# Attention heads: softmax denominator applied to the mixed values, and the mixing product turned around

## The chip, the cores and the metric

The kernel runs on one core of a Trainium2 chip. The core has five engines with a queue of instructions each: PE (TensorE, the matrix unit), DVE (VectorE), ACT (ScalarE), POOL (GpSimd) and SP (SyncE, which here only starts DMAs). The metric is the device time of one execution in microseconds (us), and less is better.

## What is computed

The reference is a trunk of four layers on 256 tokens of width 2048: an S5 state-space mixer, a squared-ReLU MLP of width 8192, windowed attention with 32 query heads and 4 key/value heads of width 64, and a second MLP. Only the attention's core is touched:

```python
scores = jnp.einsum('bnqhgd,bnkhd->bnhgqk', q, k_win).astype(jnp.float32) * scale
...
sink_b = sink.astype(jnp.float32).reshape(1, 1, N_KV_HEADS, GQA_GROUP, 1, 1)
m = jnp.maximum(jnp.max(scores, axis=-1, keepdims=True), sink_b)
p = jnp.exp(scores - m)
denom = jnp.sum(p, axis=-1, keepdims=True) + jnp.exp(sink_b - m)
probs = (p / denom).astype(h.dtype)
out = jnp.einsum('bnhgqk,bnkhd->bnqhgd', probs, v_win)
return out.reshape(bsz, seq, q_w) @ w_o
```

Each query row of each head has one denominator, the sum of its exponentials with that of the head's sink logit. The weights, divided by it, mix the value vectors `v_win`, and the 32 heads' results, side by side, are multiplied with the output matrix `w_o`. As the denominator is the same for all keys of a row, the division can be made on the weights, before the mixing, or on the mixed vector, after it.

## The kernel before, in words

All large products are made in fp32r in three parts (`mm3`, lines 642 to 648): a high half of the activations with the high half of the weights, the low half with it, and the high half with the low half of the weights. Each is one instruction with 128 stationary columns and 512 moving ones; they are called mains here. Weights are streamed: `wload` (L618 to L629) starts a DMA into one of two raw buffers (L622), ACT rounds a copy (the high half, L627), and DVE or POOL subtracts it (the low half, L628), in blocks of 128x2048 or in two halves of 128x1024.

The attention layer runs from about 1139 to 1372 us. Its main work is the query projection, four groups g of 8 heads with 16 slots each (`mains` in `attn_`), and after them the output projection; a slot is 6 mains. Token tiles tt are two of 128 tokens. The work of a group's heads is cut into stages by `attn_head` and spread over the slots of the following group by the table `HS` (L28): for each tt the slot, counted from the group's start, at which each stage is written down. After that a scheduler (Tile's) sets each engine's order from its model of the times; so a stage can stand some slots away from where the table puts it.

The stages of one group and tile:

- `rot`: squares (ACT L945), their sums (DVE L947, L948), a reciprocal root (L189 to L198, L951), and the rotary embedding, DVE L936 and L937 from the projection's bank and POOL L938.
- `turn`: PE transposes the queries (L969), ACT copies them (L971).
- `scores`: 4 products for half of the heads (L980), and DVE adds the mask and takes the row maximum out of the same bank (L984).
- `soft`: DVE L993 to L996, ACT's exponential of 8 heads with their sums (L999), DVE's denominator and its reciprocal (L1000, L1001), and 8 multiplications of the weights `sm` (128 tokens x 256 keys) by it (L1003).
- `flip`, for a pair of heads: 4 PE transposes of the weights (L1009) and ACT's copy `pT` (L1011), keys on the partitions.
- `mix`, for a pair: 4 products (L1018), stationary the values of 64 columns, moving the 128 tokens of `pT`. The result has the head's 64 channels on partitions, the upper head in partitions 64 to 127. After the fourth pair ACT rounds the bank into `aT` (L1023) and DVE writes the low half (L1024), the form in which the output projection needs it.

The 8 banks of PSUM are taken in turn (`bank`, L181): a product that begins a new bank waits until the last reader of that bank's earlier content is done. An fp32 product and an fp32 transpose show as two records each in the trace, so "x8" in the rows is four of them.

Of the kernel before, what the change touches and what calls it, by code (L numbers as in the profile page):

```python
# [9 lines left out]
F32 = mybir.dt.float32  # L10
# [6 lines left out]
P = 128  # L17
# [7 lines left out]
EPS = 1e-6  # L25
KQ = ((0, 1, 2, 3), (0, 1, 2, 3))
NEG = -1e30
HS = ((0, 5, 6, 7, 12, 13, 14, 15, 16), (1, 9, 10, 11, 19, 20, 21, 22, 23))  # L28


OT = 0.2
# [136 lines left out]
class Kernel:  # L168
# [785 lines left out]
    def attn_head(self, pool, g, banks):  # L954

        nc, v, a, pe = self.nc, self.nc.vector, self.nc.scalar, self.nc.tensor
        kT, vt = self.kT, self.vt

        def stages(tt):
            s = {}  # L960

            def rot():
                s["r"] = self.head_r(pool, banks[tt], 8, tt, 0.125, "r8")
                s["q"] = self.rope(pool, banks[tt], 8, 0, tt)

            def turn():
                bk = self.bank()
                for j in range(4):
                    pe.transpose(bk[:, j * P:(j + 1) * P], s["q"][:, j * P:(j + 1) * P], self.ident)  # L969
                s["qT"] = pool.tile([P, 4, P], F32, name="qT")  # L970
                a.copy(s["qT"].rearrange("p h c -> p (h c)"), bk)  # L971
                s["sm"] = pool.tile([P, 8, L], F32, name="sm")
                s["mx"] = self.small.tile([P, 8], F32, name="mx")

            def scores(hq):
                bks = [self.bank() for _ in range(2)]
                for i in range(2):
                    for j in range(2):
                        c = slice(j * 64, (j + 1) * 64)
                        pe.matmul(bks[j][:, i * L:(i + 1) * L], lhsT=s["qT"][c, 2 * hq + i], rhs=kT[c, g], start=True, stop=True)  # L980
                for i in range(2):
                    for j in range(2):
                        h = 2 * (2 * hq + i) + j
                        v.tensor_tensor_reduce(out=s["sm"][:, h], in0=bks[j][:, i * L:(i + 1) * L], in1=self.bias[:, tt],  # L984
                                               scale=1.0, scalar=-3.0e38, op0=ALU.add, op1=ALU.max, accum_out=s["mx"][:, h:h + 1])

            def soft():
                mx, sm = s["mx"], s["sm"]
                snk = self.sink[:, g * 8:(g + 1) * 8]
                nm = self.small.tile([P, 8], F32, name="nm")  # L990
                es = self.small.tile([P, 8], F32, name="es")
                den = self.small.tile([P, 8], F32, name="den")
                v.tensor_mul(mx, mx, s["r"])  # L993
                v.tensor_max(mx, mx, snk)
                v.tensor_scalar_mul(nm, mx, -1.0)
                v.tensor_add(es, snk, nm)  # L996
                a.activation(es, es, AF.Exp)
                for h in range(8):
                    a.activation(sm[:, h], sm[:, h], AF.Exp, scale=s["r"][:, h:h + 1], bias=nm[:, h:h + 1], accum_out=den[:, h:h + 1])  # L999
                v.tensor_add(den, den, es)  # L1000
                v.reciprocal(den, den)  # L1001
                for h in range(8):
                    v.tensor_scalar_mul(sm[:, h], sm[:, h], den[:, h:h + 1])  # L1003

            def flip(hp):
                bk = self.bank()
                for j in range(2):
                    for kt in range(2):
                        pe.transpose(bk[:, (2 * j + kt) * P:(2 * j + kt + 1) * P], s["sm"][:, 2 * hp + j, kt * P:(kt + 1) * P], self.ident)  # L1009
                pT = s["pT", hp] = pool.tile([P, 2, 2, P], F32, name="pT")  # L1010
                a.copy(pT.rearrange("p a b c -> p (a b c)"), bk)  # L1011

            def mix(hp):
                if hp == 0:
                    s["ob"] = self.bank()
                for j in range(2):
                    for kt in range(2):
                        pe.matmul(s["ob"][j * 64:(j + 1) * 64, hp * P:(hp + 1) * P], lhsT=vt[:, kt, g * 64:(g + 1) * 64],  # L1018
                                  rhs=s["pT", hp][:, j, kt], start=(kt == 0), stop=(kt == 1))
                if hp == 3:  # L1020
                    o = self.aT[:, g * 4:(g + 1) * 4, :, tt * P:(tt + 1) * P]
                    ov = s["ob"].rearrange("p (h c) -> p h c", h=4)
                    a.copy(o[:, :, 0], ov)  # L1023
                    v.tensor_sub(o[:, :, 1], ov, o[:, :, 0].bitcast(F32))  # L1024
            return [rot, turn, lambda: scores(0), lambda: (scores(1), soft()),
                    lambda: (flip(0), flip(1)), lambda: (mix(0), flip(2)), lambda: (mix(1), flip(3)), lambda: mix(2), lambda: mix(3)]
        return stages(0), stages(1)

    def proj(self, x, bk, kts, k0, kn):
# [14 lines left out]
    def attn_(self, pool, fin):  # L1044
# [56 lines left out]
        for i, _ in enumerate(mains()):  # L1101
            if i in (1, 2):
                keys(i - 1)
            for tt in range(2):
                for k, at in enumerate(HS[tt]):
                    g, r = divmod(i - 16 - at, 16)
# [246 lines left out]
```

## Time and profile before

| | |
|---|---|
| median of 3 runs | 2124.61 us (2124.23 to 2127.13) |
| profiled execution, its own time | 2126.57 us |
| its span, first to last instruction | 2124.8 us |
| mean granted clock of PE in it | 0.986 |
| attention layer in the span | about 1139 to 1372 us |

Times in the rows count from the span's start. A PE record's duration includes the pipeline, so successive records overlap; what a matmul costs is the step from its start to the next one's start. The granted clock is a share of the full 2.4 GHz; the only other level is 1.2 GHz, so 0.5 in a row or a mean below 1 says how long the lower level held.

### The profile page before, as it was taken

How to read it: one execution, taken by the hardware profiler on the slowest of the kernel's cores; microseconds unless marked ns; L12 is line 12 of the kernel's file. 1: busy time of each engine (PE TensorE's matmuls, PEld its weight loads, DVE VectorE, ACT ScalarE, POOL GpSimd, SP SyncE). 2: the span in 40 equal slices, each digit the busy share in tenths (PEclk: the TensorE clock that was granted, in tenths of full speed). 3: DMA queues.
4: the chain of work that ended last, by engine and by line, in shares of the span. 5: the costliest groups of instructions: out<-in, count | busy, mean ns of one | idle time of the engine just before them, and what ended most of it. 6: DMA issues, size and time to landing. Idle time of an engine off the chain costs nothing.

```text
span 2124.8 us, 33046 instructions
## 1 busy us (share of the span) xinstructions
PE 2034.0 (96%) x13844; PEld 1706.7 (80%) x13844; DVE 1255.5 (59%) x1820; ACT 996.3 (47%) x1233; POOL 334.5 (16%) x245
## 2 busy tenths in 40 slices
PE   3987999999999999999999889999999999999999
PEld 2876778788888888888888667788888888888887
DVE  6899746755555555444457787565555555444444
ACT  5664564444444444433445555545444444344432
POOL 5995850300000000000003340100000000000000
PEclk9998999999999999999999999999999999999999
DMA  3233446455555555655554333255555555555554
GB/s 110 61 95 104 150 175 222 164 186 190 180 193 182 185 189 200 212 187 195 205 194 147 124 119 120 104 196 206 182 195 189 188 197 182 198 196 198 191 188 156
DMA packets 59685, 364.28 MB, mean 171 GB/s; under 512 B 6816, under 2 KB 9152, under 8 KB 19600
## 3 DMA queue, kind: packets, MB, share of 16 engines
q1 hardware_dynamic: 54144, 342.32, 46.3%
q10 hardware_dynamic: 5184, 19.49, 2.8%
q8 instruction: 108, 1.77, 0.3%
q14 instruction: 41, 0.34, 0.0%
q0 software_dynamic: 208, 0.36, 0.0%
HBM read 360.05 MB, written 2.10 MB: 170 GB/s over the span
## 4 chain that ended last, share of the span: by engine, by line
PE 73%; DVE 4%; ACT 2%; DMA 2%; issue 1%; POOL 0%; SPq 0%; ACTq 0%; DVEq 0%
PE bank L838 32%; PE bank L787 22%; PE bank L788 11%; PE bank L646 2%; PE bank L647 2%; PE bank L648 2%; DVE slot L628 1%; ACT slot L999 1%; DMA slot<-in_wqkv 1%; ACT slot L627 1%; DVE slot L1003 1%; PE bank L1018 1%; PE bank L1009 1%; DVE slot L984 1%; DMA slot<-in_wup 0%
## 5 line engine op out<-in xcount | busy, mean ns | idle before, releaser
L628 DVE TENSOR_TENSOR slot<-slot,slot 128x2048 fp32r<-128x2048 f32 (+1 forms) x321 | 713.9, 2227 | 734.6 <-ACT slot L627 730.9
L627 ACT CAST slot<-slot 128x2048 fp32r<-128x2048 f32 (+2 forms) x357 | 623.3, 1752 | 746.4 <-PE bank L838 369.4
L787 PE MATMUL bank<-slot,slot 128*128 128x512 f32 x2048 | 719.5, 397 | 0.0
L838 PE MATMUL bank<-slot,slot 128*128 128x512 f32 x3072 | 696.7, 389 | 0.0
L838 PEld LDWEIGHTS bank<-slot,slot 128*128 128x128 f32 x3072 | 576.6, 188 | 119.6
L788 PE MATMUL bank<-slot,slot 128*128 128x256 f32 x2048 | 572.2, 280 | 0.0
L787 PEld LDWEIGHTS bank<-slot,slot 128*128 128x128 f32 x2048 | 385.3, 188 | 92.0
L788 PEld LDWEIGHTS bank<-slot,slot 128*128 128x128 f32 x2048 | 386.9, 189 | 0.3
L646 PE MATMUL bank<-slot,slot 128*128 128x512 f32 x544 | 218.4, 403 | 6.2 <-ACT slot L627 5.1
L647 PE MATMUL bank<-slot,slot 128*128 128x512 f32 x544 | 214.7, 395 | 0.0
L648 PE MATMUL bank<-slot,slot 128*128 128x512 f32 x544 | 208.0, 396 | 5.7 <-POOL slot L628 5.5
L796 ACT ACTIVATE slot<-slot 128x256 f32<-128x256 f32 x128 | 53.5, 419 | 160.4 <-DVE slot L795 160.4
L646 PEld LDWEIGHTS bank<-slot,slot 128*128 128x128 f32 x544 | 103.7, 191 | 30.8 <-ACT slot L627 6.5
L648 PEld LDWEIGHTS bank<-slot,slot 128*128 128x128 f32 x544 | 102.4, 190 | 29.3 <-POOL slot L628 7.4
L647 PEld LDWEIGHTS bank<-slot,slot 128*128 128x128 f32 x544 | 103.4, 190 | 20.7 <-issue 0.7
L628 POOL TENSOR_TENSOR slot<-slot,slot 128x1024 fp32r<-128x1024 f32 (+2 forms) x36 | 101.0, 2822 | 105.3 <-ACT slot L627 94.3
L909 POOL DMA_DIRECT2D slot<-in_pos x1 | 0.8, 754 | 612.7 <-DVE slot L831 612.7
L483 PE MATMUL bank<-ident,slot 128*128 128x128 f32 x256 | 37.2, 295 | 22.3 <-DVE slot L467 16.0
L505 DVE TENSOR_TENSOR bank<-bank,slot 128x256 f32<-128x256 f32 x126 | 54.4, 432 | 4.2
L795 DVE SCALAR_TENSOR_TENSOR slot<-slot 128x256 f32<-128x256 f32 x128 | 54.2, 425 | 4.2
L664 POOL TENSOR_TENSOR slot<-slot 128x512 f32<-128x512 f32 x16 | 28.9, 1813 | 171.6 <-DVE slot L1117 62.5
L830 ACT CAST slot<-slot 128x256 fp32r<-128x256 f32 x128 | 50.7, 397 | 8.0 <-PE bank L838 7.9
(210 smaller groups left out, 1442.4 us busy)
## 6 DMA issues: line engine op xcount, KB each, us to landing
slot<-in_wup SPq DMA_DIRECT2D x128, 1024.0 KB, 4.8
slot<-in_wdn SPq DMA_DIRECT2D x128, 1024.0 KB, 4.9
slot<-in_wqkv SPq DMA_DIRECT2D x20, 1024.0 KB, 4.9
slot<-in_wge ACTq DMA_DIRECT2D x32, 512.0 KB, 3.9
slot<-in_wgl SPq DMA_DIRECT2D x16, 1024.0 KB, 5.4
slot<-in_wo SPq DMA_DIRECT2D x16, 1024.0 KB, 5.0
slot<-in_bz SPq DMA_DIRECT2D x16, 336.0 KB, 3.1
slot<-in_cp SPq DMA_DIRECT2D x16, 256.0 KB, 2.9
```

Source lines behind the costliest of these rows:

```text
L505: yield v.tensor_mul(xy, lb, st[:, k - 1].rearrange("p r (o g) -> p r o g", o=1).broadcast_to([P, 2, 2, n]))
L627: self.nc.scalar.copy(hi[:, c], raw[:, c])
L628: (self.nc.gpsimd if e == "g" else self.nc.vector).tensor_sub(lo[:, c], raw[:, c], hi[:, c].bitcast(F32))
L646: pe.matmul(out, lhsT=xh, rhs=wh, start=first, stop=False)
L647: pe.matmul(out, lhsT=xl, rhs=wh, start=False, stop=False)
L648: pe.matmul(out, lhsT=xh, rhs=wl, start=False, stop=last)
L787: pe.matmul(bk, lhsT=wh[:, kt], rhs=act[:, kt].rearrange("p x c -> p (x c)"), start=(kt == 0), stop=False)
L788: pe.matmul(bk[:, :L], lhsT=wl[:, kt], rhs=act[:, kt, 0], start=False, stop=(kt == KT - 1))
L795: nc.vector.scalar_tensor_tensor(s, s, 0.0, rb, op0=ALU.max, op1=ALU.mult)
L796: nc.scalar.activation(hT(fb), s, AF.Square)
L830: nc.scalar.copy(hh, hT(kt))
L838: pe.matmul(bks[tt][cb], lhsT=x[:, ts], rhs=w[:, cb * 512:(cb + 1) * 512], start=(kt == 0 and w is wh and x is hh), stop=(kt == NK - 1 and ...
```

## The change

The 8 multiplications of the weights go. The reciprocal denominator is kept, and after the fourth `mix` one DVE instruction multiplies the bank of mixed values by it, broadcast over each head's 64 channels, into a new tile `o` (L1022). The products of `mix` swap their operands: stationary is now `pT` (128 tokens), moving the 64 columns of the values, so tokens are on the partitions and 8 heads of 64 columns fill the bank. A new stage `back` turns `o` with 4 PE transposes (L1028) into the same bank, and ACT and DVE write `aT` from there as before (L1031, L1032). The table gets a tenth entry for `back`, and some entries move by one.

```diff
--- before.py
+++ after.py
@@ -25,7 +25,7 @@
 EPS = 1e-6
 KQ = ((0, 1, 2, 3), (0, 1, 2, 3))
 NEG = -1e30
-HS = ((0, 5, 6, 7, 12, 13, 14, 15, 16), (1, 9, 10, 11, 19, 20, 21, 22, 23))
+HS = ((0, 5, 6, 7, 11, 12, 13, 14, 15, 17), (1, 9, 10, 11, 18, 19, 20, 21, 22, 23))
 
 
 OT = 0.2
@@ -999,8 +999,7 @@
                     a.activation(sm[:, h], sm[:, h], AF.Exp, scale=s["r"][:, h:h + 1], bias=nm[:, h:h + 1], accum_out=den[:, h:h + 1])
                 v.tensor_add(den, den, es)
                 v.reciprocal(den, den)
-                for h in range(8):
-                    v.tensor_scalar_mul(sm[:, h], sm[:, h], den[:, h:h + 1])
+                s["den"] = den
 
             def flip(hp):
                 bk = self.bank()
@@ -1014,16 +1013,25 @@
                 if hp == 0:
                     s["ob"] = self.bank()
                 for j in range(2):
+                    h = 2 * hp + j
                     for kt in range(2):
-                        pe.matmul(s["ob"][j * 64:(j + 1) * 64, hp * P:(hp + 1) * P], lhsT=vt[:, kt, g * 64:(g + 1) * 64],
-                                  rhs=s["pT", hp][:, j, kt], start=(kt == 0), stop=(kt == 1))
+                        pe.matmul(s["ob"][:, h * 64:(h + 1) * 64], lhsT=s["pT", hp][:, j, kt], rhs=vt[:, kt, g * 64:(g + 1) * 64],
+                                  start=(kt == 0), stop=(kt == 1))
                 if hp == 3:
-                    o = self.aT[:, g * 4:(g + 1) * 4, :, tt * P:(tt + 1) * P]
-                    ov = s["ob"].rearrange("p (h c) -> p h c", h=4)
-                    a.copy(o[:, :, 0], ov)
-                    v.tensor_sub(o[:, :, 1], ov, o[:, :, 0].bitcast(F32))
+                    s["o"] = pool.tile([P, 8, 64], F32, name="o")
+                    v.tensor_mul(s["o"], s["ob"].rearrange("p (h c) -> p h c", h=8),
+                                 s["den"].rearrange("p (h o) -> p h o", o=1).broadcast_to([P, 8, 64]))
+
+            def back():
+                bk = s["ob"]
+                for j in range(4):
+                    pe.transpose(bk[:, j * P:(j + 1) * P], s["o"][:, 2 * j:2 * j + 2].rearrange("p h c -> p (h c)"), self.ident)
+                o = self.aT[:, g * 4:(g + 1) * 4, :, tt * P:(tt + 1) * P]
+                ov = bk.rearrange("p (h c) -> p h c", h=4)
+                a.copy(o[:, :, 0], ov)
+                v.tensor_sub(o[:, :, 1], ov, o[:, :, 0].bitcast(F32))
             return [rot, turn, lambda: scores(0), lambda: (scores(1), soft()),
-                    lambda: (flip(0), flip(1)), lambda: (mix(0), flip(2)), lambda: (mix(1), flip(3)), lambda: mix(2), lambda: mix(3)]
+                    lambda: (flip(0), flip(1)), lambda: (mix(0), flip(2)), lambda: (mix(1), flip(3)), lambda: mix(2), lambda: mix(3), back]
         return stages(0), stages(1)
 
     def proj(self, x, bk, kts, k0, kn):
```

The order of three places as the scheduler now has it. A name such as bank_10111 is one use of a bank; slot39936_4589 holds the weights `sm`, slot44032_4590 and slot48128_79 hold `pT` and small tiles. First PE, the first tile of group 1 (at about 1245 to 1259 us before). Before:

```order
L980 MATMUL bank_10074<-slot44032_4590,slot49664_9557 128x256
L980 MATMUL bank_10075<-slot44032_4590,slot49664_9557 128x256
...
L1009 MATMUL bank_10121<-ident_64,slot39936_4589 128x128 x4
L1009 MATMUL bank_10127<-ident_64,slot39936_4589 128x128 x4
...
L1018 MATMUL bank_10139<-slot44032_4590 64x128 x4
L1009 MATMUL bank_10144<-ident_64,slot39936_4589 128x128 x4
L1009 MATMUL bank_10160<-ident_64,slot39936_4589 128x128 x4
```

After:

```order
L1008 MATMUL bank_10060<-ident_64,slot39936_4589 128x128 x4
L1008 MATMUL bank_10066<-ident_64,slot39936_4589 128x128 x4
L980 MATMUL bank_10072<-slot44032_4590,slot49664_9557 128x256
L980 MATMUL bank_10073<-slot44032_4590,slot49664_9557 128x256
...
L1018 MATMUL bank_10111<-slot44032_4590 128x64 x4
L1008 MATMUL bank_10116<-ident_64,slot39936_4589 128x128 x4
L1018 MATMUL bank_10111<-slot44032_4590,slot48128_79 128x64 x4
L1008 MATMUL bank_10132<-ident_64,slot39936_4589 128x128 x4
```

Before, ten mains stood between the other tile's score products and the transposes of the weights (L1009), and four more ahead of the first mixing product (L1018). Now the transposes (L1008) stand between the two halves of the score products, and the mixing follows directly.

Second DVE at the same place, from the denominator on. Before:

```order
L1000 TENSOR_TENSOR den_10000<-den_10000,es_9999 128x8
L1001 RECIPROCAL den_10000<-den_10000 128x8
L1003 TENSOR_SCALAR slot39936_4589<-slot39936_4589,den_10000 128x256 x8
L984 ISA slot39936_4589,mx_10051<-bank_10058,slot44032_4590 128x256
...
L628 TENSOR_TENSOR slot13312_2825<-slot19456_82,slot7168_4056 128x1024
...
L947 TENSOR_REDUCE hms_10188<-slot0_73 128x8
L936 TENSOR_TENSOR slot48128_79<-bank_9828,slot44032_4590 128x512
L937 TENSOR_TENSOR slot49664_9557<-bank_9828,slot44032_4590 128x512
```

After:

```order
L1000 TENSOR_TENSOR den_9994<-den_9994,es_9993 128x8
L1001 RECIPROCAL den_9994<-den_9994 128x8
L628 TENSOR_TENSOR slot13312_2825<-slot19456_82,slot7168_4056 128x1024
L947 TENSOR_REDUCE hms_10171<-slot0_73 128x8
L936 TENSOR_TENSOR slot48128_79<-bank_9817,slot44032_4590 128x512
L937 TENSOR_TENSOR slot49664_9557<-bank_9817,slot44032_4590 128x512
L628 TENSOR_TENSOR slot13312_2825<-slot19456_82,slot7168_4056 128x1024
```

The scalings L1003 are gone, and the scores' L984, which came next, now stand behind a half of a weight block (L628), the rotary embedding of the next group's first tile (L947, L936, L937 of bank_9817) and the other half. In the new order L1018's bank_10111 is the one that bank_9817 held: its first product waits for this L937, where before the first product of bank_10139 waited for the L984 of the bank that it took over.

Third the new `back`, the first tile of group 0. PE after:

```order
L1018 MATMUL bank_9906<-slot44032_4590 128x64 x4
L1008 MATMUL bank_9911<-ident_64,slot39936_4589 128x128 x4
...
L1008 MATMUL bank_9932<-ident_64,slot39936_4589 128x128 x2
L1018 MATMUL bank_9906<-slot44032_4590,slot48128_79 128x64 x4
L1028 MATMUL bank_9769<-ident_64,slot49664_9557 128x128 x4
L1008 MATMUL bank_9932<-ident_64,slot39936_4589 128x128 x2
```

DVE after, up to the multiply that L1028 waits for:

```order
L628 TENSOR_TENSOR slot15360_2826<-slot19456_82,slot7168_4056 128x1024
L947 TENSOR_REDUCE hms_9862<-slot0_73 128x8
L936 TENSOR_TENSOR slot48128_79<-bank_9529,slot44032_4590 128x512
L189 TENSOR_SCALAR slot44032_4590<-hms_9829 128x8
L190 TENSOR_SCALAR rs_h_9832<-hms_9829 128x8
L1022 TENSOR_TENSOR slot49664_9557<-bank_9769,den_9658 128x512
L937 TENSOR_TENSOR slot49664_9557<-bank_9529,slot44032_4590 128x512
```

The four transposes L1028 stand behind the second tile's transposes and mixing (bank_9906), and the multiply L1022 of bank_9769 stands on DVE behind a half L628, L947 and L936 of the next group.

## Rows read from the trace of the kernel before

**Rows 1.** The page's first part: busy us, share of the span, instructions, by engine.

```profile
PE 2034.0 (96%) x13844; PEld 1706.7 (80%) x13844; DVE 1255.5 (59%) x1820; ACT 996.3 (47%) x1233; POOL 334.5 (16%) x245
```

**Rows 2.** Windows: stretch, its length, busy us (count) of PE, PEld, DVE, ACT, POOL, granted clock.

```profile
1209.00:1310.00 101.00, 90.90 (x544) 69.32 (x543) 78.47 (x236) 57.85 (x120) 30.38 (x10) 0.95 0.35 126
1310.00:1372.00 62.00, 61.83 (x378) 48.33 (x377) 33.92 (x98) 35.95 (x77) 1.29 (x1) 1.00 0.29 103
```

**Rows 3.** Waits of PE from 1195 to 1372 us: total us, times, longest.

```profile
PE bank L1018 <- DVE mx L984: 4.7, 1, 4.7
PE bank L1009 <- DVE slot L1003: 4.1, 2, 2.5
```

**Rows 4.** Timeline near 1300 us: start, duration, engine, line; in brackets idle before, releaser.

```profile
1298.37 2.19 DVE L1003 TENSOR_SCALAR slot<-slot,den 128x256 f32<-128x256 f32 x8
1300.83 0.94 PE L1018 MATMUL bank<-slot 128*64 128x128 f32 x8 [0.84 <-ACT slot L1011]
```

**Rows 5.** Windows of 10 us, columns as in group 2.

```profile
1260.00:1270.00 10.00, 10.00 (x46) 7.92 (x45) 9.79 (x32) 7.30 (x20) 3.57 (x2) 0.82 0.46 167
1300.00:1310.00 10.00, 9.17 (x52) 7.01 (x53) 9.83 (x30) 3.67 (x10) 4.51 (x2) 0.83 0.33 107
```

**Rows 6.** Lines of DVE, 1139 to 1372 us: shapes, count, busy us, mean ns.

```profile
L1003 DVE TENSOR_SCALAR slot<-slot,den 128x256 f32<-128x256 f32 x64 | 30.4, 550 | 0.2
L1024 DVE TENSOR_TENSOR slot<-bank,slot 128x512 fp32r<-128x512 f32 x8 | 5.5, 686 | 3.0 <-ACT slot L1023 3.0
```

**Rows 7.** Timeline of PE from 1214 to 1217 us.

```profile
1214.04 0.39 PE L648 MATMUL bank<-slot,slot 128*128 128x512 f32 x1
1214.36 0.66 PE L1018 MATMUL bank<-slot 128*64 128x128 f32 x8
...
1216.54 0.47 PE L646 MATMUL bank<-slot,slot 128*128 128x512 f32 x1
```

**Rows 8.** Chain of waits, 1310 to 1372 us: start, us taken, what.

```profile
1310.09 0.23 PE bank L647
1317.76 0.87 PE bank L1009 x8
1324.53 1.93 PE bank L980 x16
1347.17 0.44 PE bank L1009 x4
```

**Rows 9.** Timeline of PE near 1428 us, where the second MLP runs.

```profile
1427.89 0.61 PE L694 MATMUL bank<-dg,ones 128*128 128x128 f32 x4
1428.25 0.48 PE L787 MATMUL bank<-slot,slot 128*128 128x512 f32 x1
1428.57 0.28 PE L788 MATMUL bank<-slot,slot 128*128 128x256 f32 x1
```

**Rows 10.** Timeline of PEld, the weight loads, at 1344 us.

```profile
1344.28 0.42 PEld L1018 LDWEIGHTS bank<-slot 128*64 128x64 f32 x8 [0.35 <-issue]
```

**Rows 11.** Timeline from 1250 to 1259 us.

```profile
1250.55 2.83 ACT L627 CAST slot<-slot 128x2048 fp32r<-128x2048 f32 x2
1251.12 6.47 DVE L1003 TENSOR_SCALAR slot<-slot,den 128x256 f32<-128x256 f32 x8
1251.62 1.15 PE L1009 MATMUL bank<-ident,slot 128*128 128x128 f32 x8 [1.62 <-DVE slot L1003]
1252.56 4.61 POOL L628 TENSOR_TENSOR slot<-slot,slot 128x2048 fp32r<-128x2048 f32 x1 [11.76 <-ACT slot L627]
1258.42 1.13 PE L1018 MATMUL bank<-slot 128*64 128x128 f32 x8 [4.72 <-DVE mx L984]
```

**Rows 12.** Timeline of DVE and POOL from 1220 to 1223 us.

```profile
1220.07 1.22 DVE L628 TENSOR_TENSOR slot<-slot,slot 128x1024 fp32r<-128x1024 f32 x1
1220.66 5.07 POOL L628 TENSOR_TENSOR slot<-slot,slot 128x2048 fp32r<-128x2048 f32 x1 [13.01 <-ACT slot L627]
1222.99 3.82 DVE L628 TENSOR_TENSOR slot<-slot,slot 128x1024 fp32r<-128x1024 f32 x1
```

## The prediction

> **What bounds the kernel now.** I read the engines' shares first: PE is busy 96% of the span and DVE 59% [rows 1]. So time is won only where PE gets less to do or stops waiting; DVE time by itself is worth nothing. The change touches one stage, attention, so I cut that into stretches. From 1209 to 1310 us PE is busy 90.90 of 101.00 us at a mean granted clock of 0.95; from 1310 to 1372, where the last heads overlap the output projection, it is busy 61.83 of 62.00 at 1.00, and DVE only 33.92 [rows 2]. In the second stretch the scaling of the weights is hidden already, and taking it out gives nothing there.
>
> Then the waits of PE: 4.7 us for DVE's L984 (one wait) and 4.1 us for L1003 (two) [rows 3], and 0.84 us for ACT's copy of turned weights [rows 4]. That is 9.6 us, all that is to be had from waits. Last the clock: its mean is 0.82 in the 10 us from 1260 and 0.83 in those from 1300, and PE is busy for most of both [rows 5]. As it is granted at 2.4 or at 1.2 GHz, 0.83 means 3.4 us at half speed, or 1.7 us of lost work; 0.82 means 1.8 us, and with the 1.6 us from PE's restart at 1258.42 to 1260, if they were at half speed too, 2.6 us. Both stretches come right behind the waits. So 9.6 + 2.6 + 1.7 = 13.9 us is the most that falling waits could return.
>
> **Part 1: 64 scalings go from DVE.** L1003 runs 64 times for 30.4 us; eight multiplies of 128x512 come instead [rows 6]. L1022 reads a bank as L1024 does (686 ns), so it adds 5.5 us. DVE is relieved by about 25 us, less where L1003's blocked time only passes to the next instruction. On PE's path this counts through the waits alone (parts 4 to 6).
>
> **Part 2: the mixing with the weights stationary.** Before, a pair of heads is 8 records with 64 stationary columns and 128 moving ones. Their price includes the steps into and out of that shape: from the main matmul at 1214.04 to the one at 1216.54 pass 2.50 us, with one main step, two mixes (the first is shown) and behind each four transposes [rows 7]. A main step is 0.23 and eight transposes are 0.87 [rows 8], so 1.40 us stay, 0.70 for a mix. After, the 8 records have 128 stationary columns and 64 moving. No row has that pair. The nearest is the transpose, also with a new block of 128 columns each time: 0.87/8 = 109 ns [rows 8]. An ordinary fp32 product of that width keeps the same pace: four records hold the stream from 1427.89 to 1428.25 and make the step after them 0.09 us longer (0.32 where a main step is 0.23), 0.45 in all [rows 9]. The stationary side seems to set it, for at the same 128 moving columns eight loads of only 64 columns follow each other in 0.42 us, 53 ns each [rows 10]. Halving the moving columns then saves nothing. I take 109 ns: 8 x 0.109 = 0.87, +0.17 a pair, **+5.4 us** for 32 pairs. Bounds: 53 ns, should the moving side set the pace after all, gives 0.42 and -8.9 us; 0.45/4 = 113 ns gives +6.4 us.
>
> By the Trainium skill, page "TensorE: Matmul & The Clock Gate", section "Back-to-back issue gap", a sustained stream of weight loads and matmuls with 128 moving columns takes about 81 ns for each; by that a mix would be 0.65 us, the term an estimated -1.6 us, and the sum about zero. The trace has 109 ns for full-width weights [rows 8], and I go by it.
>
> **Part 3: the turn back.** Four transposes for each group and token tile, 0.44 us [rows 8], 8 times: **+3.5 us**. ACT's copy and DVE's subtraction (L1031, L1032) are those of before, moved behind it; mains on PE hide them, and without that cover the subtraction alone would cost 8 x 0.69 us. PE's work grows by 5.4 + 3.5 = **8.9 us**.
>
> **Part 4: waits that fall.** The transposes of the weights wait for ACT's exponentials now, not for DVE. L1009's 4.1 us go, the 0.84 behind the second one, and the 1.7 us lost at half speed after that: **-6.6 us**.
>
> **Part 5: the wait that stays.** At 1251 L1003 takes 6.47 us for what takes 2.19 elsewhere, while POOL's L628 runs from 1252.56 for 4.61 us [rows 4, 11]. L984 comes behind it, and the mix, whose bank L984 frees, waits 4.72 us until 1258.42. In the new order its bank comes from the next group's projection, and L937 frees it. Ahead of L937 DVE now has a half of L628, L947 and L936. The half needs ACT's second cast, done near 1254 (1250.55 and 2.83, and 0.6 for the L971 now ahead); POOL works by then. Such a half takes 1.22 us alone and 3.82 with POOL beside it [rows 12]. POOL, 0.6 later than before, ends near 1257.8, the half near 1258.3, and the three behind it take 1.8 us (1221.2 to 1222.99 in [rows 12]): free near **1260.1**. PE stood at the transposes at 1250.0 (1251.62 less 1.62 of wait); four mains now ahead (0.9), four score products now behind (8 records, 1.0 by [rows 8]) and the first group's added work, a quarter of 8.9, make it 1252.1; transposes and those products bring it to the mix at 1254.0, with (a) below near 1255. So 5.1 us of wait where 4.7 were, **+0.4**, and the half speed behind it stays.
>
> **Part 6: new waits.** (a) The first turn back needs L1022, which stands on DVE behind half an L628, L947, L936 and two small ones. Before, that half ran from 1222.99 to 1226.8 [rows 12]; with 1.2 for L947 and L936, some 1.1 for the small ones and 0.7 for L1022 it is done near 1229.7, and PE is there near 1228.5: +1.2. (b) In group 2 the first copy of turned weights stands on ACT behind L971, L1031 and two casts, one of them more than before: some 3.1 us later, of which work that PE has moved ahead covers 1.2: +1.9. (c) Six more turns back, a quarter of a microsecond each: +1.5. Together **+4.6 us**; the small ones, (b) and (c) are estimates.
>
> **Sum.** 8.9 - 6.6 + 0.4 + 4.6 = +7.3, taken as +7. The profiled execution took 2126.57 us, 2.0 above the median of 2124.61; so 2133.6 against it, and as a median about **2131 us** (rounded down from 2131.6, for (c) is the softest term). A measurement of this kernel can tell about 0.2% (4.2 us) from no change.
>
> **Rivals.**
> *Faster, waits fall.* The waits fall and none replaces them. It decides if L937 is done before PE comes to the mix, that is if POOL's L628 ends before about 1254. For it: DVE has 25 us less to do and is what PE waits for in 8.8 of 9.6 us [rows 3]. Against: POOL's L628 hangs on ACT's cast, not on L1003. Then 8.9 - 13.9 = -5.0: **2119.6**. Chance 0.13.
> *Faster, PE itself.* The moving side sets the pace, 53 ns a record, 14.3 us less than forecast: **2117**. Rows 8 and 9 speak against it. 0.05.
> *No change.* Half of parts 5 and 6 is not there, because DVE's earlier scores bring the exponentials forward too: 7 - 6 = +1, **2125.6**. 0.26.
> *Much slower.* Every turn back waits, L1022 being behind a half of L628 with POOL beside it. That half takes 2.6 us more than alone [rows 12]; half of this for each of 8, and 1 us at half speed behind one, is 11 us more: **2142**. For it: PE reaches the turn back only 2 to 3 us after the mix. Against: after 1310 POOL works 1.29 us of 62 [rows 2]. 0.12.
> *The forecast*, 2127 to 2137: 0.44.
>
> **How the numbers follow.** To hold 8 in 10 I take **2118 to 2141**, which leaves out PE's own gain, a third of the falling waits and most of the much slower case. Slower by over 0.2% (above 2128.9): 0.40 of the forecast's 0.44, the 0.12, and 0.02 from the edge of no change, 0.54. Faster (below 2120.4): 0.05 and 0.11 of 0.13, 0.16. Within: 0.30.
>
> **What would show it.** In the changed profile: 8 records of L1018 in about 0.87 us; 4 of L1028 in 0.44; no L1003, and 5.5 us of L1022; a wait of L1018 for L937 near 1255 to 1260 while POOL's L628 runs; waits of L1028 for L1022. I am wrong if L1018 takes about 0.45, if there is no such wait for L937, or if PE's waits in the stage come to over 20 us.

## The result and the profile after

The changed kernel takes 2132.85 us (median of 15 runs), beside 2125.69 us of the kernel before in the same session: a ratio of 1.0033, 95% interval 1.0025 to 1.0041. That is some 7 us more, where 6.4 had been forecast (2131.0 against 2124.61). Sign and size were right. Two of the terms behind the sum were not, and one reason given for a right number was wrong.

The page of the profile after, first part, has the same share of PE and 15 us less of DVE [rows 1]:

```profile
PE 2042.2 (96%) x13876; PEld 1723.5 (81%) x13876; DVE 1240.1 (58%) x1764; ACT 996.7 (47%) x1233; POOL 331.5 (16%) x245
```

The time was lost inside the attention layer. Its first main and the first product of the MLP behind it, in the timeline of PE before, and then after (start, duration):

```profile
1127.50 0.50 PE L646 MATMUL bank<-slot,slot 128*128 128x512 f32 x1 [1.01 <-ACT slot L676]
...
1415.68 0.48 PE L787 MATMUL bank<-slot,slot 128*128 128x512 f32 x1
```

```profile
1127.26 0.50 PE L646 MATMUL bank<-slot,slot 128*128 128x512 f32 x1 [1.01 <-ACT slot L676]
...
1422.15 0.48 PE L787 MATMUL bank<-slot,slot 128*128 128x512 f32 x1
```

From one to the other pass 288.18 us before and 294.89 after, +6.71. The spans differ by 6.5 (2124.8 and 2131.3): next to nothing is gained or lost elsewhere. Between these two marks lies what is called the layer below.

The waits of PE from 1195 us on, after, against [rows 3, 4]:

```profile
PE bank L1018 <- DVE slot L937: 5.2, 1, 5.2
PE bank L646 <- ACT slot L627: 3.5, 1, 3.5
PE bank L1028 <- DVE slot L1022: 1.0, 1, 1.0
PE bank L980 <- DVE slot L1032: 0.4, 1, 0.4
PE bank L647 <- DVE slot L1032: 0.2, 1, 0.2
```

No wait for L1003 is left, and the wait of the mix has changed its releaser from L984 to L937 and grown from 4.7 to 5.2 us. The wait for ACT's L627 stood there before, too (3.5 us). The chain of waits after, from 1310 us:

```profile
1326.43 1.11 PE bank L980 x8
1343.18 0.84 PE bank L1018 x8
1359.72 0.44 PE bank L1028 x4
```

A mix of two heads is now 0.84 us in the chain, where part 2 had forecast 0.87 for 0.70; the turn back (L1028) is 0.44; the score products L980 come in eights at 1.11, where before sixteen took 1.93 [rows 8]. The windows after, for [rows 2, 5]:

```profile
1139.00:1209.00 70.00, 63.10 (x282) 49.76 (x280) 48.61 (x106) 31.23 (x45) 26.66 (x12) 0.93 0.37 133
1209.00:1310.00 101.00, 94.46 (x559) 79.53 (x556) 66.87 (x191) 55.66 (x113) 26.61 (x10) 0.97 0.34 122
1260.00:1270.00 10.00, 9.77 (x48) 9.10 (x49) 9.40 (x40) 3.07 (x10) 3.48 (x2) 0.68 0.45 165
1300.00:1310.00 10.00, 10.00 (x75) 8.68 (x72) 10.00 (x30) 3.91 (x6) 1.36 (x2) 1.00 0.55 181
```

In the 101 us from 1209 PE is busy 3.6 us more than before; the clock is lower for longer near 1260 (0.68 for 0.82) and no longer near 1300 (1.00 for 0.83).

Last the two places that the forecast worked out, the first turn back and the mix of group 1 [rows 11], in the timeline after:

```profile
1228.85 0.68 DVE L1022 TENSOR_TENSOR slot<-bank,den 128x512 f32<-128x512 f32 x1
1229.58 0.66 PE L1028 MATMUL bank<-ident,slot 128*128 128x128 f32 x4 [0.96 <-DVE slot L1022]
...
1250.65 2.84 ACT L627 CAST slot<-slot 128x2048 fp32r<-128x2048 f32 x2
1252.68 4.53 POOL L628 TENSOR_TENSOR slot<-slot,slot 128x2048 fp32r<-128x2048 f32 x1 [16.67 <-ACT slot L627]
1253.53 4.77 DVE L628 TENSOR_TENSOR slot<-slot,slot 128x1024 fp32r<-128x1024 f32 x1 [2.81 <-ACT slot L627]
1259.41 0.68 DVE L937 TENSOR_TENSOR slot<-bank,slot 128x512 f32<-128x512 f32 x1
1260.23 1.94 PE L1018 MATMUL bank<-slot 128*128 128x64 f32 x8 [5.20 <-DVE slot L937]
```

L1022 ends at 1229.53 and L1028 starts 0.96 us late. At the second place DVE's half of L628 takes 4.77 us while POOL's block runs beside it (no_pool below shows it without); it ends near 1258.3, L937 at 1259.41 + 0.68 = 1260.09, and PE goes on at 1260.23.

### The profile page after: what moved, and what is told of

Its sections match the earlier page's. It is cut to its first block, busy times and chain, and to the rows that moved or that the text cites. A ratio compares the mean times of both kernels' runs of the same rounds, so it can differ in the third digit from the quotient of the medians.

```text
span 2131.3 us, 33058 instructions
## 1 busy us (share of the span) xinstructions
PE 2042.2 (96%) x13876; PEld 1723.5 (81%) x13876; DVE 1240.1 (58%) x1764; ACT 996.7 (47%) x1233; POOL 331.5 (16%) x245
## 4 chain that ended last, share of the span: by engine, by line
PE 76%; DVE 3%; ACT 1%; DMA 1%; issue 1%; POOL 0%; SPq 0%; ACTq 0%; DVEq 0%
PE bank L838 32%; PE bank L787 22%; PE bank L788 11%; PE bank L646 2%; PE bank L648 2%; PE bank L647 2%; DVE slot L628 1%; PE bank L1018 1%; ACT slot L627 1%; DMA slot<-in_wqkv 1%; PE bank L1008 1%; PE bank L980 0%; DMA slot<-in_wgl 0%; ACT slot L999 0%; PE bank L673 0%
## 5 line engine op out<-in xcount | busy, mean ns | idle before, releaser
L628 DVE TENSOR_TENSOR slot<-slot,slot 128x2048 fp32r<-128x2048 f32 (+1 forms) x321 | 718.1, 2239 | 742.0 <-ACT slot L627 741.8
L627 ACT CAST slot<-slot 128x2048 fp32r<-128x2048 f32 (+2 forms) x357 | 623.5, 1753 | 740.0 <-PE bank L838 361.7
L628 POOL TENSOR_TENSOR slot<-slot,slot 128x1024 fp32r<-128x1024 f32 (+2 forms) x36 | 100.5, 2805 | 112.0 <-ACT slot L627 108.9
```

What stands on the lines that cost most here:

```text
L627: self.nc.scalar.copy(hi[:, c], raw[:, c])
L628: (self.nc.gpsimd if e == "g" else self.nc.vector).tensor_sub(lo[:, c], raw[:, c], hi[:, c].bitcast(F32))
```

## The experiments

All times are medians beside runs of the kernel before on the same chip; "PE time" of a kind of record is the sum, over the trace, from each record's start to the next one's start, waits left out; it is taken at whatever clock was granted, unless the full clock is named.

**What a record of the mixing costs.** The forecast said that the 128 stationary columns set 109 ns a record, and that 64 stationary columns go at 53. Three kernels issue each product again, so that its price shows as a difference.

```diff
 # mix_twice: the changed kernel; mix_twice_32 with 32 in place of 64
+                    for kt in range(2):
+                        pe.matmul(s["ob"][:, h * 64:h * 64 + 64], lhsT=s["pT", hp][:, j, kt], rhs=vt[:, kt, g * 64:g * 64 + 64],
+                                  start=(kt == 0), stop=(kt == 1))
 # old_mix_twice: the kernel before, inside the loop over j
+                    for kt in range(2):
+                        pe.matmul(s["ob"][j * 64:(j + 1) * 64, hp * P:(hp + 1) * P], lhsT=vt[:, kt, g * 64:(g + 1) * 64],
+                                  rhs=s["pT", hp][:, j, kt], start=(kt == 0), stop=(kt == 1))
```

> The changed kernel with every mixing product issued a second time, writing the same values again: 128 more fp32 products, 256 records. If the 128 stationary columns set the pace (109 ns a record), PE gets 27.9 us more and the time is about 35 us above the kernel before (some 2160). If the 64 moving columns did, at 53 ns, it is 13.6 us more, 21 above before (some 2146).

> As the run with the mixing twice, but the second issue moves only 32 columns. If the stationary side sets the pace, nothing is saved by this: within 2 us of that run (some 2160). If the moving side does, half of the added time goes, 7 to 14 us less than that run.

> The kernel before with every mixing product issued twice, 64 stationary columns and 128 moving: 256 more records. If the stationary columns set the pace, 53 ns each, 13.6 us above the kernel before (some 2139). If a record costs 109 ns in either shape, 28 us above it (some 2153).

Measured: 2153.05 us (ratio 1.0128, 1.0114 to 1.0141), 2156.38 (1.0142, 1.0126 to 1.0158) and 2147.18 (1.0110, 1.0087 to 1.0133). The chain of mix_twice, and then of mix_twice_32 (L1021 is the second issue):

```profile
1356.06 0.45 PE bank L1021 x4
1356.51 0.45 PE bank L1018 x4
```

```profile
1357.68 0.42 PE bank L1021 x4
1358.10 0.47 PE bank L1018 x4
```

Four records take 0.45 us with 64 moving columns and 0.42 with 32: the moving side is not what sets the pace at these widths. By PE time the added records cost 29.5 us at 64 and 28.0 at 32. In total time mix_twice came out between the two theories (20 us more than the changed kernel, by the differences to the kernel before, where 27.9 and 13.6 us of PE work were in question), and mix_twice_32 another 3 us up. Most of what is short of 27.9 lies in PE's waits, which fell in the layer from 13.7 to 8.4 us. In both runs the mix no longer waits for L937: in mix_twice it starts at 1258.03 us, before L937 (1260.53). The bank that L937 frees has gone to the transposes L1008 behind it, which wait 1.2 us. In total time alone mix_twice would not have told the theories apart; the chain does.

The third fell out against the forecast's reason. The added records cost 28 us of PE time (L1018 and L1021 together 48.7 us, L1018 alone 20.6 before), 109 ns each, though their stationary side has 64 columns. The timeline of PE in that run shows why:

```profile
1358.63 0.27 PE L1021 MATMUL bank<-slot 128*64 128x128 f32 x1
1358.64 0.32 PE L1018 MATMUL bank<-slot 128*64 128x128 f32 x1
1358.74 0.27 PE L1021 MATMUL bank<-slot 128*64 128x128 f32 x1
1358.80 0.27 PE L1018 MATMUL bank<-slot 128*64 128x128 f32 x1
1358.85 0.27 PE L1021 MATMUL bank<-slot 128*64 128x128 f32 x1
1358.91 0.27 PE L1018 MATMUL bank<-slot 128*64 128x128 f32 x1
```

L1021 is still the first head, L1018 already the second. Each of the two goes on in steps of 0.11 us (one of 0.16), and their starts lie between each other's. The two heads of a pair write partitions 0 to 63 and 64 to 127, and PE works on both at once, each in its half of the columns. In the kernel before that went through all eight records, so 0.42 us were four steps of 0.11 with two records in each. The Trainium skill has the rule, on the page "TensorEngine Tiling (Array Packing)", section "Key Properties": tiles of the array are independent, and different tiles can load weights and multiply in parallel. The rows above agree: 0.01 to 0.10 us lie between starts, where 0.11 is the step of one head.

To test it, the repeat was placed so that the heads alternate in blocks of four records:

```diff
 # old_mix_twice_alt: the kernel before
                 for j in range(2):
                     for kt in range(2):
                         pe.matmul(s["ob"][j * 64:(j + 1) * 64, hp * P:(hp + 1) * P], lhsT=vt[:, kt, g * 64:(g + 1) * 64],
                                   rhs=s["pT", hp][:, j, kt], start=(kt == 0), stop=(kt == 1))
+                for j in range(2):
+                    for kt in range(2):
+                        pe.matmul(s["ob"][j * 64:(j + 1) * 64, hp * P:(hp + 1) * P], lhsT=vt[:, kt, g * 64:(g + 1) * 64],
+                                  rhs=s["pT", hp][:, j, kt], start=(kt == 0), stop=(kt == 1))
```

> The kernel before with the mixing of a pair issued a second time behind the first, so that blocks of four records alternate between the two heads (in the earlier run all eight of one head came first, and 256 records added 28 us of PE time). If the two heads of a pair run side by side, one in each half of PE's columns, while the blocks alternate, the added records cost half: 14 us above the kernel before (some 2139 to 2142). If a record simply costs 109 ns in that shape, about 25 us above it (some 2150).

Measured: 2139.51 us (1.0063, 1.0041 to 1.0085). The chain:

```profile
1352.74 0.59 PE bank L1018 x8
1353.33 0.48 PE bank L1022 x8
```

The added eight records (L1022) take 0.48 us, not 0.88. The same 256 records cost 13 us here and 22 in the run before, in PE time 15 and 28: working side by side is shown.

**The same device in the new arrangement.** If halves of the columns work at once, the turned product can be split by tokens:

```diff
 # mix_halves: the changed kernel
                     for kt in range(2):
-                        pe.matmul(s["ob"][:, h * 64:(h + 1) * 64], lhsT=s["pT", hp][:, j, kt], rhs=vt[:, kt, g * 64:(g + 1) * 64],
-                                  start=(kt == 0), stop=(kt == 1))
+                        for t in (slice(0, 64), slice(64, P)):
+                            pe.matmul(s["ob"][t, h * 64:(h + 1) * 64], lhsT=s["pT", hp][:, j, kt, t], rhs=vt[:, kt, g * 64:(g + 1) * 64],
+                                      start=(kt == 0), stop=(kt == 1))
```

> The changed kernel with each mixing product split by tokens: 64 stationary columns, and the two token halves written to the two halves of the partitions, twice as many products. If halves run side by side, a pair of heads takes 8 steps of 55 to 109 ns in place of 8 of 109: 0 to 14 us less than the changed kernel, 2119 to 2133, nearer the lower end if 64 moving columns are cheap once the weights are narrow. If they don't run side by side, 256 more records of 55 to 109 ns: 2133 to 2161.

Measured: 2128.84 us (1.0011, 0.9999 to 1.0023), 2.5 us above the kernel before where the changed kernel is 7.2. The chain:

```profile
1344.79 1.08 PE bank L1019 x32
```

Thirty-two records, two pairs of heads, take 1.08 us: 0.54 a pair against 0.84, with twice the instructions. PE time of the mixing falls from 29.5 to 20.3 us. Of these 9.1 us half came back as waits: those of PE in the layer rose from 13.7 to 18.1 us, with 5.9 for L937 (5.2 before the split), 2.0 for the turn back (1.0), 1.7 for L971, 1.7 for POOL's L938 (0.2) and 0.7 for L984.

**The turn back alone.**

```diff
 # no_turn: the changed kernel; the turn is left out, and L1022's quotient is not used
-                for j in range(4):
-                    pe.transpose(bk[:, j * P:(j + 1) * P], s["o"][:, 2 * j:2 * j + 2].rearrange("p h c -> p (h c)"), self.ident)
```

> The changed kernel without the four transposes that turn the mixed values back; ACT and DVE write the unturned and undivided bank, so turn and division are left out of the output. If the turn costs what the trace shows, 32 transposes x 110 ns and the 1.0 us wait for L1022, the time falls by 4.5 us against the changed kernel, to 2.5 us above the kernel before. If it were hidden, the time stays 7 us above it.

Measured: 2127.75 us (1.0003, 0.9994 to 1.0013), 2.3 us above the kernel before and so some 5 under the changed one. DVE's division still runs in it (eight L1022, 5.5 us), so it is PE's part alone that went. The turn back is on PE's path, as forecast.

**What taking L1003 away is worth by itself.**

```diff
 # no_scaling: the kernel before
-                for h in range(8):
-                    v.tensor_scalar_mul(sm[:, h], sm[:, h], den[:, h:h + 1])
```

> The kernel before without the 64 scalings of the weights (the division is left out altogether), nothing else changed: what taking L1003 from DVE is worth by itself. By the waits that name L1003 (4.1 us, 0.8 behind them, 1.7 of half speed) 6.6 us less than before, some 2119; up to 13.9 less (2112) if the wait for L984 goes too; no change if the waits only move to the next instruction on DVE.

Measured: 2123.13 us (0.9987, 0.9972 to 1.0002): some 3 us, with an interval from 6 less to none: under half of the 6.6 that was expected, and not clear of zero. The waits of PE in that run from 1195 us on:

```profile
PE bank L1016 <- ACT slot L1009: 8.8, 2, 5.2
PE bank L646 <- ACT slot L627: 3.5, 1, 3.5
```

L1016 is the mixing, L1009 there ACT's copy of the turned weights. Without L1003 PE is early at the mix and waits 8.8 us for ACT, whose queue has the exponentials and two casts ahead of the copy; before, the two mixing waits and L1003's were 9.6. So 30 us of DVE work were worth little to PE: behind them stands ACT.

**POOL's block beside DVE's.** The block of low halves that POOL computes near 1252 us was given to DVE (QH is the table of who computes which block; "g" is POOL).

```diff
 # no_pool: the changed kernel; before_no_pool: the same line in the kernel before
-QH = ("v", "vv", "vv", "v") + ("vv", "g") * 8
+QH = ("v", "vv", "vv", "v") + ("vv", "g") * 6 + ("vv", "v", "vv", "g")
```

> The changed kernel with one block of low halves (the one that POOL computes near 1252 us) given to DVE. If POOL's work beside DVE is what makes L937 late, half the L628 of 1024 takes 1.2 us in place of 4.8, L937 is done near 1258, and the wait of 5.2 us shrinks to about 1: 4 to 7 us less than the changed kernel, 2126 to 2129. If DVE's own queue is the cause, the extra 2.3 us on DVE make it worse: 2133 to 2136.

> The kernel before with the same block of low halves moved from POOL to DVE, to see whether the change is needed for that gain. If POOL's block is what makes L1003 slow near 1251 us, L1003 takes about 2.2 us in place of 6.5, the wait of 4.7 us for L984 goes or nearly goes, and the time falls by 4 to 7 us, to 2119 to 2122. If DVE, with its 64 scalings, has no room for the block, no gain or a loss.

Measured: 2128.56 us (1.0008, 0.9994 to 1.0022) for the changed kernel, some 5 us less; 2137.47 (1.0050, 1.0037 to 1.0064) for the kernel before, 12 us more. The waits of no_pool, then of before_no_pool:

```profile
PE bank L1018 <- ACT slot L1010: 1.1, 1, 1.1
PE bank L1028 <- DVE slot L1022: 1.0, 1, 1.0
```

```profile
PE bank L1009 <- DVE slot L1003: 13.4, 2, 11.7
PE bank L1018 <- DVE mx L984: 0.4, 1, 0.4
```

In the changed kernel the wait for L937 is gone and 1.1 us for ACT's copy stand in its place. In the profiled execution the layer takes 289.9 us, 5.0 less than in the changed kernel (the rest of it took 6 us more, so its span is no shorter), and the clock stays at 1.00 from 1250 to 1270. POOL's block is one part of the cause, the place of a bank the other. The timeline of no_pool, and then of no_turn:

```profile
1251.81 3.43 DVE L628 TENSOR_TENSOR slot<-slot,slot 128x2048 fp32r<-128x2048 f32 x2 [1.87 <-ACT slot L627]
1255.35 1.10 PE L1018 MATMUL bank<-slot 128*128 128x64 f32 x8 [1.11 <-ACT slot L1010]
1256.35 0.68 DVE L937 TENSOR_TENSOR slot<-bank,slot 128x512 f32<-128x512 f32 x1
```

```profile
1253.73 4.75 DVE L628 TENSOR_TENSOR slot<-slot,slot 128x1024 fp32r<-128x1024 f32 x1 [2.81 <-ACT slot L627]
1259.59 0.68 DVE L937 TENSOR_TENSOR slot<-bank,slot 128x512 f32<-128x512 f32 x1
1260.32 1.11 PE L1008 MATMUL bank<-ident,slot 128*128 128x128 f32 x4 [2.49 <-DVE slot L937]
```

Without POOL beside it DVE does the whole block and the half behind it in 3.43 us, and L937 is done at 1257.03, 3.1 us earlier than in the changed kernel. But the mix starts before that: the bank that L937 frees has gone to the transposes L1008 behind the mix, as in no_turn, where POOL's block is in place and L1008 waits 2.5 us for it. Had the mix kept that bank in no_pool, it would have waited from 1254.24 to 1257.03, an estimated 2.8 us. So of the 5.2 us POOL's block explains some 2.4 by itself.

In the kernel before the same move takes the 4.7 us for L984 away (0.4 left), and L1003 takes 2.19 us at 1251 as expected; but later one wait of 11.7 us for L1003 appears, with the clock at 1.2 GHz around it:

```profile
1292.00:1315.00 23.00, 8.29 (x37) 6.32 (x38) 20.74 (x84) 12.27 (x39) 2.55 (x2) 0.50 0.27 92
```

So the place that was looked at got better and the next group got worse. The trace shows where. The exponentials wait for DVE's L995, which stands at 1302.09 us, 7.7 behind L993 (1294.37), with a rotary embedding, row maxima and a block L628 of 2.28 us (1298.35) between them; in the kernel before L995 follows L993 after 0.4 us (1291.89 and 1292.28). PE has 8 mains between the turn of the queries (L969) and the next 16 score records to cover this, where it had 21. So moving one block also changed the scheduler's order, and the 12 us are the price of both.

**Towards a kernel that beats both.** Three kernels put these together, all with mix_halves: with no_pool's line; with all eight blocks taken from POOL; and with POOL as it was, but the first tile's stages one slot later.

```diff
 # mix_halves_pool_none
-QH = ("v", "vv", "vv", "v") + ("vv", "g") * 8
+QH = ("v", "vv", "vv", "v") + ("vv", "v") * 8
 # mix_halves_later
-HS = ((0, 5, 6, 7, 11, 12, 13, 14, 15, 17), (1, 9, 10, 11, 18, 19, 20, 21, 22, 23))
+HS = ((0, 5, 6, 7, 12, 13, 14, 15, 16, 18), (1, 9, 10, 11, 18, 19, 20, 21, 22, 23))
```

> The changed kernel with the mixing in token halves and the block near 1252 us on DVE. Each alone gave about 5 us; if they act on different things (PE's work, one wait of PE) they add: 2122 to 2125, at or a little under the kernel before. If the wait for L937 only gives way to another one, 2127 to 2130.

> The same with all eight blocks of the query projection taken from POOL and given to DVE, which the change relieved by 25 us. If POOL's blocks cost more by what they block on DVE than they save, PE's waits for POOL's L628 (3.3 us near 1170 and 1187) go too: 2118 to 2123. If DVE becomes late with the low halves, PE waits for L628 on DVE instead: 2127 or more.

> The changed kernel with the mixing in token halves, POOL's blocks as they were, and the first tile's stages from the transposes of the weights on one slot later, as in the table before. If the place in the order is what put L937 ahead of the mix, the wait of 5.9 us falls and the time with it, 2122 to 2126. If POOL's block beside DVE is the cause, some other instruction of DVE behind it is waited for, and the time stays near 2129.

Measured: 2123.54 us (0.9990, 0.9982 to 0.9999), 2107.52 (0.9913, 0.9899 to 0.9926) and 2119.09 (0.9963, 0.9950 to 0.9975). The first two gains add, about as expected. The second is the best kernel of this study, 18 us under the kernel before and 25 under the changed one. Its windows and the only wait of PE that its trace lists from 1130 to 1400 us:

```profile
1139.00:1209.00 70.00, 70.00 (x360) 56.40 (x359) 50.57 (x129) 37.62 (x52) 10.17 (x9) 1.00 0.50 184
1209.00:1310.00 101.00, 100.37 (x813) 78.34 (x811) 73.85 (x229) 66.21 (x148) 8.92 (x6) 1.00 0.33 116
```

```profile
PE bank L980 <- ACT slot L971: 1.7, 1, 1.7
```

PE is busy throughout and the clock is 1.00 all the way, also from 1139 to 1209, where the changed kernel had 0.93 and 63.10 us busy of 70; DVE took over eight blocks of 2.3 us and its busy time in the layer is still lower than in mix_halves, 179.5 us for 186.2, as POOL no longer holds it up. The third was expected to keep its wait if POOL was the cause; it lost it (2.8 us for ACT's copy are left) and came out lower than either theory had it, so the place in the order matters as well as POOL. How much of the changed kernel's own 7 us lies in the places that its table HS gives the stages was not run with the full-width mixing and stays open. Whether the kernel before would gain as much with no block on POOL at all wasn't tried.

## Why the prediction was right, point by point

- **Part 1** (DVE relieved by 25 us): L1003 is gone, L1022 takes 5.5 us as forecast, and DVE's total fell by 15.4 us (1255.5 to 1240.1). The rest went where the forecast said it might: other instructions are held up by POOL in L1003's place, the half of L628 for 4.77 us among them.
- **Part 2** (mixing, +5.4): the size was right, the reason was not. At the full clock PE time of L1018 rose from 77 to 109 ns a record, +8.2 us over 256; the transposes beside it, which had paid for the step between shapes, fell from 118 to 104 ns (128 of them, -1.7) and those of the queries by 0.6. Net +5.9. But "the stationary side seems to set it", read from eight loads in 0.42 us, was a wrong reading: those were two heads side by side, and a single head's records take 109 ns with 64 stationary columns too. The lower bound of 53 ns for one full-width record had no ground in that row.
- **Part 3** (turn back, +3.5): 32 transposes at 110 ns, 3.5 us; leaving them out gave some 5 with the wait.
- **Part 4** (waits that fall, -6.6): the 4.1 and 0.84 us and the stretch at half speed near 1300 are gone. The change takes them away; no_scaling shows that removing L1003 alone would not have, for there ACT's copy is waited for instead. The forecast called 9.6 us all that was to be had from waits. PE waited 17.6 us in the layer, with 4.1 for POOL's L628 and 3.5 for ACT's L627 that it left out, and mix_halves_pool_none has 1.7 left.
- **Part 5** (the wait that stays, 5.1 us until 1260.1): 5.2 us until 1260.1, with POOL's block and the half of L628 where they were placed. no_pool shows that this block explains about half of it, the rest being that the mix takes the bank that L937 frees. What was short is the clock behind it: the 10 us from 1260 lost 3.2 us (0.68), where 2.6 were taken over from before.
- **Part 6** (new waits, +4.6): (a) 1.0 us for 1.2, with L1022 done at 1229.5 for 1229.7. (b) was wrong: no wait of PE stands in group 2, which is busy in all 10 us from 1300. (c) 0.6 us for 1.5, in two waits for L1032.
- **What was not in the sum:** the score products. In the new order 128 records of L980 are cut into more, shorter runs between other shapes, mostly eights where sixteens stood, and their PE time at the full clock rose from 126 to 142 ns a record: +2.1 us. Some 0.6 of it is of another kind, a run of sixteen near 1237 us that stops in its middle for L1032. The order had shown the shorter runs, and no price was put on them.

By the traces: PE's work at the full clock 5.9 + 3.5 + 2.1 = +11.5 (8.9 forecast); PE's waits in the layer 17.6 before and 13.7 after, -3.9, of which 0.8 at POOL's L628, which the change does not touch; the clock some -0.9 (17.8 us of PE's work ran at half speed before, 15.9 after). Together +6.7, and 6.71 were measured. So 2.6 us too little work and 3.0 us too much of new waits (part 6) cancelled: the sum was better than its terms, and that it came so close was luck.

## What to carry to other kernels

A busy engine beside the bound one is worth nothing by its hours: 30 us taken from DVE changed the time by some 3 us, because ACT stood behind the same mix. Before a matmul is turned around, look at the starts of single records, not at their sum: if two of them lie closer together than one's own step, the old form uses the array's two halves at once, and the new form must be split in the same way to keep that. A transfer of work between engines is to be priced by what it blocks: eight blocks less on POOL, on top of the split, were worth 21 us, and one block less in the other kernel cost 12. Such an edit also moves the scheduler's order and the banks, so which instruction waits for which is to be read again in each run's trace, before its time is put down to the block.

## What was not expected of the hardware

- fp32 records with a full 128 stationary columns take 109 to 112 ns (0.45 us for four) at 64 moving columns, and 0.42 us for four at 32. With 64 stationary columns and 128 moving, one head alone takes 109, too, and two heads in the two column halves take it together.
- With 64 stationary and 64 moving columns, 32 records in the two halves take 1.08 us, 34 ns each with the steps into and out of that shape.
- DVE's half of a block (128x1024, both inputs and the output in SBUF) takes 1.22 us where it begins 0.6 us ahead of POOL's block, and 3.82 and 4.77 us where it begins behind it [rows 12, and the changed kernel near 1253]; both times it ends 1.1 us after POOL's block.
- Behind PE's wait of 5.2 us the granted clock averaged 0.68 over 10 us; in the kernel whose longest wait in the layer was 1.7 us it stayed at 1.00 throughout.
